# A ring of four raw weight chunks in place of three, and 37 universal tiles in place of 39

## The chip, the cores and the metric

The kernel runs on one core of a Trainium2 chip. A core has five engines that run side by side, each through its own queue of instructions: TensorE (PE, matrix products), VectorE (DVE), ScalarE (ACT), GpSimd (POOL) and SyncE (SP), which here only starts transfers (DMAs). They meet through semaphores: an instruction waits until what it reads has been written and what it overwrites has been read. On-chip memory is SBUF (128 partitions) and PSUM (eight banks, into which TensorE adds up). The metric is the time of one execution in microseconds (us); lower is better.

## The reference

A decoder trunk of two layers on 512 tokens of width 1024, in float32. Each layer has a mixer and a gated feed-forward network (FFN), each between two RMS norms:

```python
for i in range(DEPTH):                       # DEPTH = 2
    h = rms_norm(x, norm_g[i, 0])
    if i % 2 == 0:                           # differential attention and a short gated convolution
        p = h @ w_in_even[j]
        ...
        mix = jnp.concatenate([a_out, b_out], axis=-1) @ w_out_even[j]
    else:                                    # spatial gating unit
        mix = spatial_gating(h, w_in_odd[j], ..., w_out_odd[j])
    x = x + rms_norm(mix, norm_g[i, 1])
    h = rms_norm(x, norm_g[i, 2])
    f = (jax.nn.silu(h @ w_gate[i]) * (h @ w_up[i])) @ w_down[i]   # 1024 -> 2816 -> 1024
    x = x + rms_norm(f, norm_g[i, 3])
```

All weights lie in device memory and are read once.

## The kernel before, in words

**Weights.** SyncE loads all weights as chunks of at most 8 KB a partition (1 MB) into a ring of tiles `raw` (pool `rawp`, L83), in one fixed list `chunks`. `load` (L307 to L321) issues chunks until a limit of chunks whose parts have not all been read is met (L310). Chunks of the FFN are two transfers, a half of w_gate and a half of w_up, 512 KB each. A load can start once the tile that it takes over has been read, so a load waits for the release of the chunk that stood in that tile.

**Split.** Every weight piece is split into two reduced-precision parts: ScalarE casts the high part `whi` (L135), VectorE subtracts it from the raw piece to make the low part `wlo` (L136). TensorE then makes three products for each product wanted: high with high, high with low, low with high.

**FFN.** Gate and up are done in 11 units of 256 columns by a scheme with seven products in place of eight: the unit has two chunks ("a" and "b"), VectorE makes sums of their quarters (`wsum`, L263), and 7 pieces are multiplied, each 24 matmuls of 128x256 (L679). Results are combined on VectorE (L754, a PSUM bank and a copied tile, L759 on ScalarE makes the copy), then silu (L764, ScalarE) and the product (L765, VectorE) give `hidden`. The first three units start with two small pieces each, before all tokens are ready. The next use of a PSUM bank by TensorE can wait for the addition of L754. GpSimd in the meantime issues transfers that add up sums of w_down in device memory (`tsum`, L186), paced by L779; the down projection then runs on these in the same scheme.

**Pools.** The pool `ap` (tag "a", 4 KB a partition a tile) is shared by whi, wlo, wsum, the normed and turned activations, `hidden` and norm vectors. An allocation that finds all tiles in use waits for the reader of the oldest fitting one. Ring and pool together take 3 x 8 + 39 x 4 = 180 KB a partition.

**Order.** A scheduler sets the order on each engine when the kernel is built, from its own estimates of time; ScalarE's and VectorE's order is written out in the prologue alone, GpSimd's in the FFN. SyncE's queue follows the order in which loads are issued in the code.

Of the kernel before, what the change touches and what calls it, by code (L numbers as in the profile page):

```python
# [72 lines left out]
def trunk(  # L73
# [6 lines left out]
    nc = tc.nc  # L80
    pool = lambda name, bufs, **kw: ctx.enter_context(tc.tile_pool(name=name, bufs=bufs, **kw))
    const = pool("const", 1)
    rawp = pool("rawp", 3)  # L83
    ap_ = pool("ap", 39)
    tp = pool("tp", 8)
    sp = pool("sp", 24)
    ps_ = pool("ps", 8, space=bass.MemoryType.PSUM)
# [4 lines left out]
    def nm(base):  # L92
        n_made[0] += 1
        return f"{base}_{n_made[0]}"
# [19 lines left out]
    chunks, order = [], []  # L114
# [86 lines left out]
    class Unit:  # L201
# [46 lines left out]
        def sum(self, s):  # L248
            if s in self.sums:
                return self.sums[s]  # L250
            for before in self.NEEDS.get(s, []):
                self.sum(before)
            t = ap_.tile([P, 2, 4, P], F32, tag="a", name=nm("wsum"))
            if s == "s1":
                x, y, op = self.quarter("a", 1), self.quarter("b", 1), ALU.add
            elif s == "s2":
                x, y, op = self.sums["s1"], self.quarter("a", 0), ALU.subtract
            elif s == "s3":
                x = self.half["a"].tile[:, :, :, 0:P]
                y, op = self.quarter("a", 1), ALU.subtract  # L260
            else:
                x, y, op = self.quarter("b", 0), self.sums["s2"], ALU.subtract
            nc.vector.tensor_tensor(out=t, in0=x, in1=y, op=op)  # L263
            self.sums[s] = t
            return t
# [39 lines left out]
    n_loaded, n_split, ready = [0], [0], []  # L305

    def load(upto=1000):  # L307

        while n_loaded[0] < min(upto, len(chunks)):
            if sum(c.left > 0 for c in chunks[:n_loaded[0]]) >= 3:  # L310
                return
            c = chunks[n_loaded[0]]
            c.tile = rawp.tile(c.shape, F32, tag="raw", name=nm("raw"),
                               padded_shape=[P, 2048 // math.prod(c.shape[2:])] + c.shape[2:])
            for part, view in c.views:
                if n_loaded[0] >= 2:
                    nc.sync.dma_start(out=c.tile[part], in_=view)
                else:
                    for ks in (slice(0, 2), slice(2, 4)):
                        nc.sync.dma_start(out=c.tile[:, ks, :], in_=view[:, ks, :])  # L320
            n_loaded[0] += 1  # L321

    def ahead(n):

        while len(ready) < n and n_split[0] < len(order):
            key, need, make = order[n_split[0]]
            load()
            assert all(c.tile is not None for c in need)
            ready.append((key, make()))
            n_split[0] += 1  # L330
            load()
# [493 lines left out]
    for t in range(1, NT):  # L825
        load(t)
        nc.sync.dma_start(out=xs[t], in_=x[0, t * P:(t + 1) * P, :])
    with tc.manual_schedule(engines={mybir.EngineType.Activation, mybir.EngineType.DVE}):
# [62 lines left out]
        for i in range(2):  # L891
# [3 lines left out]
                            ap=[[1, P], [STRIP, 2], [1, 512]]))  # L895
# [298 lines left out]
```

## Time and profile before

| what | us |
|---|---|
| median of 3 runs (1069.45 to 1069.95) | 1069.6 |
| the profiled execution | 1071.01 |
| its span, first to last instruction | 1069.1 |
| TensorE busy in it | 1034.5 (97%) |
| VectorE busy | 812.6 (76%) |
| ScalarE busy | 552.1 (52%) |
| GpSimd busy | 191.4 (18%) |

The mean granted clock of TensorE is 0.99. The profiled execution lies 1.4 us above the median of the runs; its span leaves 1.9 us around it. The FFN's products run from 233 to 474 us in layer 0 and from 722 to 959 us in layer 1; in layer 0 the down projection follows until the second layer's mixer starts, in layer 1 it ends the kernel. In the timelines a number in brackets is the idle time of the engine just before an instruction, and behind the arrow stands what ended it. A matmul's duration overlaps with the next one's; what counts is the distance of two starts.

### The profile page before, as it was taken

Reading aid. Unit: us, or ns where it says so; the run is one execution under the profiler, and the core shown is the slowest. Engines: PE = TensorE matmul, PEld = TensorE weight load, DVE = VectorE, ACT = ScalarE, POOL = GpSimd, SP = SyncE. Lnnn points to the kernel's source line nnn. Section 1 sums busy time; section 2 is a strip of 40 time slices with the busy share of each in tenths; the row PEclk is TensorE's granted clock in tenths of the full one; section 3 lists DMA queues with packets and bytes.
Section 4 is the critical chain, followed back from the end, with each engine's and each line's share of the span. In section 5 each row is a group of like instructions: output and inputs, shape, how many; then the busy total and the mean of one; then the engine's idle time right before and its main releaser. Section 6 shows DMA issues by size and latency. Waiting matters only on the chain.

```text
span 1069.1 us, 16311 instructions
## 1 busy us (share of the span) xinstructions
PE 1034.5 (97%) x6395; PEld 923.1 (86%) x6395; DVE 812.6 (76%) x1179; ACT 552.1 (52%) x903; POOL 191.4 (18%) x259
## 2 busy tenths in 40 slices
PE   7999999998999999999999999998899999999997
PEld 5777778887899999998888788888899999998885
DVE  4466654489887996899978454679898797799974
ACT  4456453366453553584846433356455454474842
POOL 1012220011233333220000000010334343220000
PEclk7999999999999999999999999999999999999999
DMA  9231304326788798574744522414789799774741
GB/s 324 57 119 40 119 13 169 94 81 190 191 266 220 188 279 229 159 219 144 280 148 153 163 79 79 138 51 147 207 226 273 201 273 240 177 217 148 257 175 40
DMA packets 112526, 181.10 MB, mean 169 GB/s; under 512 B 5009, under 2 KB 77854, under 8 KB 110402
## 3 DMA queue, kind: packets, MB, share of 16 engines
q1 hardware_dynamic: 96578, 133.92, 38.0%
q0 software_dynamic: 15872, 46.14, 18.7%
q8 instruction: 50, 0.82, 0.3%
q14 instruction: 26, 0.21, 0.1%
HBM read 177.94 MB, written 48.24 MB: 212 GB/s over the span
## 4 chain that ended last, share of the span: by engine, by line
PE 72%; DVE 15%; DMA 4%; ACT 3%; issue 3%; POOL 1%; SPq 0%; DVEq 0%; POOLq 0%; ACTq 0%
PE ps L109 41%; PE ps L679 28%; DVE wlo L136 5%; DMA raw<-in_w_up_dram 3%; DVE wsum L263 3%; ACT whi L135 1%; POOL s L344 1%; DVE hTlo L432 1%; DVE h L503 1%; DVE t L754 1%; ACT j L491 1%; DVE x L552 1%; PE ps L952 1%; DMA raw<-in_w_in_even_dram 1%; DVE t L438 1%
## 5 line engine op out<-in xcount | busy, mean ns | idle before, releaser
L679 PE MATMUL ps<-hThi,whi 128*128 128x256 f32 x1232 | 275.1, 285 | 8.2 <-ACT whi L135 4.9
L679 PE MATMUL ps<-hThi,wlo 128*128 128x256 f32 x1232 | 275.0, 284 | 5.1 <-DVE wlo L136 5.1
L679 PE MATMUL ps<-hTlo,whi 128*128 128x256 f32 x1232 | 274.0, 284 | 1.3 <-DVE hTlo L432 1.3
L136 DVE TENSOR_TENSOR wlo<-raw,whi 128x1024 fp32r<-128x1024 f32 (+1 forms) x206 | 239.7, 1185 | 31.7 <-ACT whi L135 30.7
L135 ACT CAST whi<-raw 128x1024 fp32r<-128x1024 f32 (+1 forms) x206 | 203.6, 1018 | 27.3 <-DMA raw<-in_w_up_dram 7.8
L679 PEld LDWEIGHTS ps<-hThi,whi 128*128 128x128 f32 x1232 | 203.6, 192 | 10.6 <-ACT whi L135 5.9
L679 PEld LDWEIGHTS ps<-hThi,wlo 128*128 128x128 f32 x1232 | 204.0, 192 | 6.6 <-DVE wlo L136 6.5
L679 PEld LDWEIGHTS ps<-hTlo,whi 128*128 128x128 f32 x1232 | 203.8, 192 | 1.9 <-DVE hTlo L432 1.9
L135 ACT CAST whi<-wsum 128x1024 fp32r<-128x1024 f32 x88 | 90.1, 1045 | 57.7 <-DVE wsum L263 50.4
L109 PE MATMUL ps<-whi,wlo 128*128 128x512 f32 x308 | 119.9, 389 | 0.0
L109 PE MATMUL ps<-wlo,whi 128*128 128x512 f32 x308 | 119.8, 389 | 0.0
L109 PE MATMUL ps<-whi,whi 128*128 128x512 f32 x308 | 119.5, 390 | 0.2 <-DVE t L719 0.2
L779 POOL TENSOR_SCALAR pace<-t 128x1 f32<-128x1 f32 x96 | 74.2, 773 | 245.9 <-ACT t L764 172.4
L136 DVE TENSOR_TENSOR wlo<-wsum,whi 128x1024 fp32r<-128x1024 f32 x88 | 105.5, 1219 | 15.9 <-ACT whi L135 15.9
L344 POOL TENSOR_TENSOR s<-s,neg_half 128x1 f32<-128x1 f32 (+1 forms) x40 | 25.0, 627 | 486.8 <-DVE s L484 415.2
L754 DVE TENSOR_TENSOR t<-ps,t 128x512 f32<-128x512 f32 x88 | 58.4, 684 | 32.8 <-ACT t L759 17.6
L759 ACT COPY t<-ps 128x512 f32<-128x512 f32 x66 | 38.5, 583 | 86.2 <-PE ps L679 86.2
L109 PE MATMUL ps<-whi,a 128*128 128x512 f32 x256 | 79.9, 391 | 0.0
L186 POOL DMA_DIRECT2D tsum<-in_w_down_dram x72 | 68.4, 953 | 2.1 <-issue 0.8
L109 PEld LDWEIGHTS ps<-whi,whi 128*128 128x128 f32 x308 | 57.8, 188 | 12.6 <-issue 0.8
L109 PEld LDWEIGHTS ps<-wlo,whi 128*128 128x128 f32 x308 | 57.8, 188 | 11.9
L109 PEld LDWEIGHTS ps<-whi,wlo 128*128 128x128 f32 x308 | 57.8, 188 | 11.9
(143 smaller groups left out, 1485.8 us busy)
## 6 DMA issues: line engine op xcount, KB each, us to landing
tsum<-in_w_down_dram POOLq DMA_DIRECT2D x60, 512.0 KB, 7.0
raw<-in_w_gate_dram SPq DMA_DIRECT2D x44, 512.0 KB, 5.8
raw<-in_w_up_dram SPq DMA_DIRECT2D x44, 512.0 KB, 7.4
raw<-tsum SPq DMA_DIRECT2D x16, 1024.0 KB, 5.0
raw<-in_w_down_dram SPq DMA_DIRECT2D x12, 1024.0 KB, 5.9
raw<-in_w_in_even_dram SPq DMA_DIRECT2D x10, 1024.0 KB, 6.7
tsum<-tsum POOLq DMA_DIRECT2D x20, 512.0 KB, 5.9
raw<-in_w_in_odd_dram SPq DMA_DIRECT2D x8, 1024.0 KB, 5.4
```

The lines of the kernel that those rows point to most:

```text
L109: nc.tensor.matmul(out, lhsT, rhs, start=start, stop=stop, **kw)
L135: nc.scalar.copy(out=hi, in_=src)
L136: nc.vector.tensor_tensor(out=lo, in0=src, in1=hi.bitcast(F32), op=ALU.subtract)
L186: return [lambda to=to, of=of, g=g, op=op: nc.gpsimd.dma_start(out=to[:, g, :], in_=of[:, g, :], accum_op=op) for g in self.PAIRS for op, ...
L263: nc.vector.tensor_tensor(out=t, in0=x, in1=y, op=op)
L344: nc.gpsimd.tensor_tensor(out=y0[:, :n], in0=a, in1=neg_half[:, :n], op=ALU.pow)
L432: nc.vector.tensor_tensor(out=self.part(1, p, t), in0=src, in1=self.part(0, p, t).bitcast(F32), op=ALU.subtract)
L438: minus = lambda out, x, y: nc.vector.tensor_tensor(out=out, in0=x, in1=y, op=ALU.subtract)
L679: nc.tensor.matmul(bank[:, m * 256:(m + 1) * 256], piece[a][:, m, k, :], hT.at(b, p)[:, k, :], start=first and m == 0 and i == 0, stop=i = ...
L754: nc.vector.tensor_tensor(out=c, in0=x, in1=y, op=ALU.add)
L759: nc.scalar.copy(out=c, in_=x)
L779: nc.gpsimd.tensor_scalar(out=pace, in0=at[:, 0:1], scalar1=1.0, scalar2=None, op0=ALU.mult)
```

## The change

The ring has four tiles, `load` lets four chunks be unread, and the universal pool has 37 tiles: 4 x 8 + 37 x 4 = 180 KB again. Nothing is computed in another way.

```diff
@@ -80,8 +80,8 @@
     nc = tc.nc
     pool = lambda name, bufs, **kw: ctx.enter_context(tc.tile_pool(name=name, bufs=bufs, **kw))
     const = pool("const", 1)
-    rawp = pool("rawp", 3)
-    ap_ = pool("ap", 39)
+    rawp = pool("rawp", 4)
+    ap_ = pool("ap", 37)
     tp = pool("tp", 8)
     sp = pool("sp", 24)
     ps_ = pool("ps", 8, space=bass.MemoryType.PSUM)
@@ -307,7 +307,7 @@
     def load(upto=1000):
 
         while n_loaded[0] < min(upto, len(chunks)):
-            if sum(c.left > 0 for c in chunks[:n_loaded[0]]) >= 3:
+            if sum(c.left > 0 for c in chunks[:n_loaded[0]]) >= 4:
                 return
             c = chunks[n_loaded[0]]
             c.tile = rawp.tile(c.shape, F32, tag="raw", name=nm("raw"),
```

What the scheduler makes of it is shown at three places. On SyncE in the prologue (raw are the weight chunks of w_in_even, rows, lam_in, table and oh the small tables, strip_d and a the attention bias), before:

```order
L853 DMA rows<-in_conv_w_dram 12x128
L317 DMA raw_180<-in_w_in_even_dram 128x8x256
L854 DMA rows<-in_diff_subln_g_dram 1x128
L863 DMA lam_in<-in_diff_lambda_dram 128x256
L879 DMA table<-in_rel_bias_dram 32x4
L881 DMA oh<-in_one_hot_dram 32x512
L317 DMA raw_208<-in_w_in_even_dram 128x8x256
L889 DMA strip_d<-strip 4x640
```

and now:

```order
L317 DMA raw_154<-in_w_in_even_dram 128x8x256
L317 DMA raw_182<-in_w_in_even_dram 128x8x256
L317 DMA raw_210<-in_w_in_even_dram 128x8x256
L853 DMA rows<-in_conv_w_dram 12x128
L854 DMA rows<-in_diff_subln_g_dram 1x128
L863 DMA lam_in<-in_diff_lambda_dram 128x256
L879 DMA table<-in_rel_bias_dram 32x4
L881 DMA oh<-in_one_hot_dram 32x512
L889 DMA strip_d<-strip 4x640
```

Three loads stand ahead of the small tables now, one of them a chunk that before came behind the bias. On SyncE at the start of layer 0's FFN (g are norm vectors, raw the halves of gate and up), before:

```order
L317 DMA raw_2106<-in_w_gate_dram 128x4x128
L317 DMA raw_2106<-in_w_up_dram 128x4x128
L360 DMA g_2194<-in_norm_g_dram 128x1024
L360 DMA g_2196<-in_norm_g_dram 128x1024
L317 DMA raw_2205<-in_w_gate_dram 128x4x256
L317 DMA raw_2205<-in_w_up_dram 128x4x256
```

and now:

```order
L317 DMA raw_2013<-in_w_gate_dram 128x4x128
L317 DMA raw_2013<-in_w_up_dram 128x4x128
L317 DMA raw_2109<-in_w_gate_dram 128x4x256
L317 DMA raw_2109<-in_w_up_dram 128x4x256
L360 DMA g_2197<-in_norm_g_dram 128x1024
L360 DMA g_2199<-in_norm_g_dram 128x1024
```

The two norm vectors come behind one more chunk. On VectorE in the eighth of the units of layer 0 (wsum sums, wlo low parts, t additions of line 754, a the hidden products), before:

```order
L263 TENSOR_TENSOR wsum_4246<-wsum_4204,raw_3797 128x1024
L136 TENSOR_TENSOR wlo_4284<-wsum_4246,whi_4283 128x1024
L263 TENSOR_TENSOR wsum_4287<-raw_4002,wsum_4246 128x1024
L754 TENSOR_TENSOR t_4232<-ps_4108,t_4230 128x512
L754 TENSOR_TENSOR t_4236<-ps_4109,t_4230 128x512
L765 TENSOR_TENSOR a_3494<-t_4232 128x256
L136 TENSOR_TENSOR wlo_4321<-wsum_4204,whi_4320 128x1024
L765 TENSOR_TENSOR a_3499<-t_4236 128x256
```

and now:

```order
L263 TENSOR_TENSOR wsum_4249<-wsum_4207,raw_3759 128x1024
L136 TENSOR_TENSOR wlo_4287<-wsum_4249,whi_4286 128x1024
L754 TENSOR_TENSOR t_4235<-ps_4111,t_4233 128x512
L754 TENSOR_TENSOR t_4239<-ps_4112,t_4233 128x512
L765 TENSOR_TENSOR a_3497<-t_4235 128x256
L263 TENSOR_TENSOR wsum_4290<-raw_3800,wsum_4249 128x1024
L765 TENSOR_TENSOR a_3502<-t_4239 128x256
L136 TENSOR_TENSOR wlo_4324<-wsum_4207,whi_4323 128x1024
```

Two additions have moved ahead of the sum of line 263, and a product ahead of a split. The same kind of exchange stands in the last units of each layer and at the start of the down projections; TensorE exchanges single matmuls there, and GpSimd's order is as it was.

## Rows read from the trace of the kernel before

**Rows 1.** The page's first section: busy us, share of span, instructions.
```profile
PE 1034.5 (97%) x6395; PEld 923.1 (86%) x6395; DVE 812.6 (76%) x1179; ACT 552.1 (52%) x903; POOL 191.4 (18%) x259
```

**Rows 2.** Waits of TensorE, 240 to 480 us: total, times, longest.
```profile
PE ps L679 <- DVE wlo L136: 2.8, 4, 0.9
PE ps L679 <- DVE t L754: 2.8, 2, 1.8
PE ps L679 <- ACT whi L135: 2.2, 2, 1.8
```

**Rows 3.** Timeline, TensorE, 303 to 312 us: start, duration, instruction, idle before and releaser.
```profile
...
304.28 0.28 PE L679 MATMUL ps<-hThi,whi 128*128 128x256 f32 x1
304.40 0.28 PE L679 MATMUL ps<-hThi,wlo 128*128 128x256 f32 x1
306.46 0.47 PE L679 MATMUL ps<-hThi,whi 128*128 128x256 f32 x1 [1.79 <-DVE t L754]
...
```

**Rows 4.** Timeline, VectorE, 292 to 308 us.
```profile
...
301.71 1.22 DVE L136 TENSOR_TENSOR wlo<-raw,whi 128x1024 fp32r<-128x1024 f32 x1 [2.49 <-ACT whi L135]
...
305.13 1.28 DVE L754 TENSOR_TENSOR t<-ps,t 128x512 f32<-128x512 f32 x2
...
```

**Rows 5.** Timeline, ScalarE, 292 to 308 us.
```profile
...
300.63 2.00 ACT L135 CAST whi<-raw 128x1024 fp32r<-128x1024 f32 x2 [2.85 <-DMA raw<-in_w_up_dram]
...
```

**Rows 6.** Timeline, SyncE's queue, 255 to 320 us.
```profile
...
280.97 0.51 SPq L317 DMA_DIRECT2D raw<-in_w_up_dram  x1
...
292.38 0.51 SPq L317 DMA_DIRECT2D raw<-in_w_up_dram  x1
...
```

**Rows 7.** Windows: busy us of PE, PEld, DVE, ACT, POOL; granted clock, DMA share, GB/s.
```profile
306.46:310.10 3.64, 3.64 (x17) 3.64 (x18) 2.88 (x4) 1.14 (x2) 1.57 (x2) 0.53 0.26 23
```

**Rows 8.** Timelines of SyncE, ScalarE, VectorE and TensorE, 350 to 394 us.
```profile
...
358.21 0.51 SPq L317 DMA_DIRECT2D raw<-in_w_up_dram  x1
...
370.30 0.51 SPq L317 DMA_DIRECT2D raw<-in_w_up_dram  x1
...
380.06 1.05 ACT L135 CAST whi<-raw 128x1024 fp32r<-128x1024 f32 x1 [2.70 <-DMA raw<-in_w_up_dram]
...
381.15 1.23 DVE L136 TENSOR_TENSOR wlo<-raw,whi 128x1024 fp32r<-128x1024 f32 x1 [1.45 <-ACT whi L135]
...
390.56 0.39 PE L679 MATMUL ps<-hThi,whi 128*128 128x256 f32 x1 [0.97 <-DVE t L754]
...
```

**Rows 9.** Timelines of ScalarE and TensorE in layer 1, 780 to 797 us.
```profile
...
789.39 2.00 ACT L135 CAST whi<-raw 128x1024 fp32r<-128x1024 f32 x2 [1.67 <-DMA raw<-in_w_up_dram]
...
795.22 0.74 PE L679 MATMUL ps<-hThi,whi 128*128 128x256 f32 x4 [0.57 <-DVE t L754]
...
```

**Rows 10.** Windows at the start of each FFN stage (columns as in 7).
```profile
245.00:280.00 35.00, 29.63 (x231) 27.99 (x232) 33.41 (x43) 18.20 (x28) 6.82 (x9) 1.00 0.58 178
...
720.00:765.00 45.00, 38.74 (x302) 36.78 (x301) 42.70 (x67) 28.21 (x49) 6.79 (x10) 1.00 0.52 164
```

**Rows 11.** Timelines of VectorE and TensorE, 282 to 288 us.
```profile
...
283.76 1.23 DVE L263 TENSOR_TENSOR wsum<-raw,raw 128x1024 f32<-128x1024 f32 x1 [0.26 <-DMA raw<-in_w_up_dram]
...
287.39 0.38 PE L679 MATMUL ps<-hThi,wlo 128*128 128x256 f32 x1 [0.88 <-DVE wlo L136]
...
```

**Rows 12.** Waits of ScalarE, 392 to 480 us.
```profile
...
ACT whi L135 <- PE ps L679: 6.5, 4, 2.6
...
```

**Rows 13.** Windows in the steady part of each FFN stage.
```profile
392.00:480.00 88.00, 88.00 (x700) 86.27 (x698) 73.66 (x86) 50.16 (x68) 25.07 (x38) 1.00 0.77 204
797.00:960.00 163.00, 163.00 (x1345) 162.28 (x1344) 138.32 (x158) 88.43 (x121) 56.87 (x77) 1.00 0.85 230
```

**Rows 14.** Timeline, VectorE, 403 to 412 us.
```profile
...
407.66 1.23 DVE L263 TENSOR_TENSOR wsum<-raw,wsum 128x1024 f32<-128x1024 f32 x1 [0.57 <-PE ps L679]
...
```

**Rows 15.** Timelines of SyncE and TensorE in the prologue.
```profile
...
21.88 0.38 SPq L317 DMA_DIRECT2D raw<-in_w_in_even_dram  x1
...
44.38 0.23 PE L856 MATMUL ps<-ident,rows 16*128 16x16 f32 x1
...
```

## The prediction

> **What bounds the kernel now.** The page's first section comes first: TensorE is busy 97% of the span, so what can be won at all is the time in which it stands still or runs at a lower clock [rows 1]. Next come the waits of TensorE in the feed-forward (FFN) stage; the reader is to see which engine ended each wait [rows 2]. In layer 0 one of the two largest groups, 2.8 us in two waits, is on the VectorE addition of line 754; the rest is on splits (whi, wlo). The list of idle stretches and their engines is only the outside of it: behind each wait I went back one engine at a time, in the timelines of TensorE, VectorE, ScalarE and SyncE, until a wait had no engine behind it. Where that ends at a DMA of raw weights, a chunk that starts one step sooner can help; where it ends at a VectorE that had no pause, it can't.
>
> The larger of the two line-754 waits: TensorE stands still for 1.79 us before 306.46 [rows 3]. The addition that it waits for starts at 305.13, behind a VectorE that had itself lost 2.49 us at 301.71 to a missing whi [rows 4], which ScalarE could not cast because the chunk's second half (in_w_up) had not landed: idle 2.85 us before 300.63 [rows 5]. That half was issued at 292.38, about 8.2 us before [rows 6]. After the stall TensorE is granted half of its clock: in the 3.64 us from 306.46 the mean grant is 0.53, and 17 matmuls are done [rows 7].
>
> The smaller: 0.97 us before 390.56 [rows 8]. ScalarE sits 2.70 us before 380.06 for in_w_up, VectorE then 1.45 us for ScalarE. The half was issued at 370.30, so it took 9.8 us [rows 8]. Layer 1 has the same picture in small: 0.57 us before 795.22, behind 1.67 us of ScalarE on in_w_up before 789.39 [rows 9].
>
> The start of both FFN stages is different. From 245 to 280 us VectorE is busy 33.41 of 35 us, and from 720 to 765 it is 42.70 of 45 us [rows 10]. TensorE's waits there are on wlo and whi that VectorE makes as fast as it can. No load changes that.
>
> **The change part by part.** *The ring.* A load now waits for the release of the chunk four before it, not three. Each FFN chunk is one of two for a unit of seven pieces, so releases come in pairs. The load issued at 292.38 therefore takes the place of the one issued at 280.97, 11.4 us sooner, and the one at 370.30 that of 358.21, 12.1 us sooner [rows 6, 8]. Even with the 9.8 us landing of the slower one they are there at about 291 and 368, before ScalarE wants them (near 297.8, which is 300.63 less 2.85, and 377.4).
>
> What is late next? At the first place VectorE can go on at 301.71 - 2.49 = 299.2; its row of work up to the addition lasts 3.4 us (301.71 to 305.13), so the two additions run from 302.6 to 303.9, where before they ended at 306.4. TensorE's last matmul before the stall starts at 304.40 and the next would follow 0.12 us later [rows 3], so 0.6 us of slack are left and the 1.79 us go whole. At the second place VectorE gains its 1.45 us, and the addition ends 0.5 us before it is due: the 0.97 us go whole [rows 8]. At the third, 1.67 us of ScalarE stand against 0.57 us: gone [rows 9].
>
> *The clock.* If the stall at 306 goes, the half-clock stretch goes with it: 17 matmuls at the spacing of 0.12 us seen just before take 2.04 us, they took 3.64, so 1.60 us [rows 3, 7]. Bounds: 0, if something else lowers it, and 1.60.
>
> The rows show a clock drop behind the 1.79 us stall, but none behind a wait of 1.8 us for whi in the FFN's start, where the grant stays 1.00 from 245 to 280 [rows 2, 10]. So the sum takes one drop. [...]
>
> *Another few tenths.* At 283.76 VectorE waits 0.26 us for in_w_up, and that passes through its chain to the 0.88 us stall at 287.39: 0.26 us [rows 11]. Bounds 0 and 0.88; the chain is VectorE's own otherwise, so the lower price.
>
> *The pool.* 37 tiles in place of 39: whi, wlo, sums and hidden share it, and an allocation waits only when all are in use. That is so at the end of the FFN: between 392 and 480 ScalarE's casts wait 6.5 us in four waits for TensorE to give a tile back [rows 12]. With two tiles fewer each such wait is for a release up to one piece (24 matmuls, 24 x 0.12 = 2.9 us) later. It costs nothing while the splits run ahead of TensorE, and they do: it is busy 88.00 of 88 us there and 163.00 of 163 in the same stretch of layer 1 [rows 13]. That row shows that the lead is above zero, not how large it is. Bounds: 0, or one piece for each of four waits, 11.5 us; I take 0, since even four waits of up to 2.6 us cost TensorE nothing today.
>
> *The order.* In the late FFN the additions of line 754 move ahead of a sum or split that waits for a tile. At 407.66 the sum (line 263) waits 0.57 us for a tile and the two additions stand behind it [rows 14]; they would start up to 1.7 us sooner, the sum some 1.3 us later (the two additions, 1.28 us in [rows 4]). TensorE waits for neither there: 0, with bounds of 1.3 us each way. At the start, three loads pass ahead of the five small tables (conv weights, bias table, one-hot). The last of them waits for the release at which SyncE issued a load before, 21.88, so the tables go out behind that, against a first use at 44.38 [rows 15]: 0, since 22 us of other matmuls lie between; it would cost only if they took longer than that. The norm vectors go behind one pair of loads, and are out when the pair's chunk has been released; that is the release at which SyncE issued a load before them, so it is 0 too. Nothing else is passed in SyncE's queue, and GpSimd's order stays.
>
> **Sum.** 1.79 + 1.60 + 0.97 + 0.57 + 0.26 = 5.19 us. The profiled execution took 1071.01 us (span 1069.1 and 1.9 around it): 1065.8. The median of the runs shown, 1069.6, lies 1.4 below the profiled one; from it, 1064.4. I forecast 1064.6.
>
> **Rivals.**
> 1. *The pool stops TensorE* (slower). Place: the last units of each FFN stage, where ScalarE already waits for tiles [rows 12]. If the lead of a piece there is under 2.9 us, TensorE gets a stall of up to 2.9 us with a clock drop of 1.6 behind it, in each layer: 2 x 4.5 = 9.0, against 5.2 gained: 1069.6 + 3.8 = 1073.4. It decides from a stall of 2.6 us per layer in all. For it: two tiles are worth one piece. Against it: TensorE's idle time there is zero.
> 2. *VectorE stays late* (same). The loads land, but VectorE, busy 84 to 95% of the FFN [rows 10, 13], is bound by sums and splits, and the two stalls come back a piece later as waits for wlo. Only the 0.57 and part of the rest are won, some 1.2 us: 1068.4. For it: the start of the stage is of that kind throughout [rows 10]. Against it: 2.49 and 1.45 us of pause that VectorE demonstrably had [rows 4, 8].
> 3. *Transfers collide* (same). The earlier load runs beside GpSimd's accumulating transfers of w_down and takes as much longer as it starts earlier. The half issued at 292.38 needed 8.2 us, the one at 370.30 9.8 us; to undo 11.4 us it would need about 20. Time: 1069.6, or slightly less. The Trainium skill ("DMA: Bandwidth & Descriptors", SWDGE vs HWDGE vs iDMA) says that the DMA engines alternate between the queues fed by GpSimd and by SyncE. By it a load beside a burst of sums is slowed to about half its rate, never held up, which fits the rows; no run here shows it alone.
> 4. *More is won* (faster). Part of the 0.88 us at 287 and of the start stalls goes too, and waits that lengthen ScalarE's chain vanish: another 3 us at most, 1061.6.
>
> **How the numbers follow.** A change under 0.2%, 2.1 us, can't be told from none here. Forecast (gain 3 to 6.5 us): 0.58. Rival 4: 0.10. Rivals 2 and 3 with gains under 2.1: 0.15 and 0.04; a small pool cost that eats most of the gain: 0.04. Rival 1: 0.09. So faster 0.69, same 0.22, slower 0.09. The range reaches from 1061.8 (rival 4) to 1070.0, which leaves out rival 1 and the far end of 4. The likeliest case's own range is 1063.1 to 1066.6.
>
> **What would show it.** Right: no TensorE wait on line 754 near 304 and 388 and none near 794; a granted clock of 1.00 through 300 to 320; ScalarE's waits for in_w_up in the FFN at nearly none; in_w_up issued near 281 and 358. Right on the pool: longer waits of ScalarE's casts for TensorE in the late FFN, and TensorE still without pause from 392 on. Wrong: any new wait of TensorE on whi or wlo between 392 and 480 or between 797 and 960, a second half-clock stretch, or landings of raw chunks of 15 us and more.

## The result and the profile after

The changed kernel takes 1064.1 us (median of 4 runs, 1062.89 to 1065.65) against 1069.78 for the kernel before (4 runs, 1069.45 to 1072.3): a ratio of 0.9944, with a 95% interval of 0.9927 to 0.9961, 5.7 us. Forecast were 1064.6. The profiled execution took 1065.65 us, its span is 1063.9; before they were 1071.01 and 1069.1.

The page's first section and the waits of TensorE from 240 to 480 us, in the order of [rows 1, 2]:

```profile
PE 1032.9 (97%) x6395; PEld 922.0 (87%) x6395; DVE 812.0 (76%) x1179; ACT 552.4 (52%) x903; POOL 199.5 (19%) x259
```

```profile
PE ps L679 <- DVE wlo L136: 2.6, 4, 0.9
PE ps L679 <- ACT whi L135: 2.2, 2, 1.8
...
```

The group on line 754 is gone, the other two stand where they stood (2.6 against 2.8 us, 2.2 against 2.2). How it went is read from the place near 306: timelines of SyncE, ScalarE, VectorE and TensorE (the places of [rows 6, 5, 4, 3]), then the window from 300 to 320 us.

```profile
...
281.62 0.51 SPq L317 DMA_DIRECT2D raw<-in_w_up_dram  x1
...
297.09 2.96 ACT L135 CAST whi<-raw 128x1024 fp32r<-128x1024 f32 x3
...
298.35 2.35 DVE L136 TENSOR_TENSOR wlo<-raw,whi 128x1024 fp32r<-128x1024 f32 x2
...
303.00 1.29 DVE L754 TENSOR_TENSOR t<-ps,t 128x512 f32<-128x512 f32 x2
...
304.75 0.28 PE L679 MATMUL ps<-hThi,wlo 128*128 128x256 f32 x1
304.87 0.28 PE L679 MATMUL ps<-hThi,whi 128*128 128x256 f32 x1
...
```

```profile
300.00:320.00 20.00, 20.00 (x169) 20.00 (x169) 19.24 (x22) 10.10 (x15) 12.52 (x14) 1.00 0.93 285
```

The half of w_up that was issued at 292.38 starts at 281.62. ScalarE casts three pieces in a row from 297.09 without a pause, VectorE goes from 298.35 to 304.3 with hardly one, and the two additions end 0.6 us before TensorE's first matmul that needs them, at 304.87, which follows its predecessor by 0.12 us. The grant is 1.00 throughout, where the same window of the kernel before has 0.91.

Start by start, the 6395 matmuls of the two profiled executions can be laid against each other. The changed kernel is 0.65 us late when the FFN begins, then gains 0.30 at 287, 1.94 at the stall near 306 (1.79 of wait and the slower first matmul), 1.60 over the next 17 matmuls, 1.24 near 390 and 0.84 near 795; all other steps are 0.11 us or less and nearly cancel. The sum is 5.9, less 0.65 makes the 5.2 by which the span is shorter.

The 0.65 us arise before 24 us, where TensorE runs at half clock in both. Executions of one kernel differ by more than that: in the two profiles of the kernel before, the FFN's first wait for h ended at 245.70 and 246.95, in the two of the changed kernel at 246.36 and 245.15.

What the pool does is in ScalarE's waits and in two windows, in the order of [rows 12, 13]:

```profile
...
ACT whi L135 <- PE ps L679: 11.2, 5, 4.2
ACT whi L135 <- PE ps L109: 2.4, 2, 1.4
...
```

```profile
392.00:480.00 88.00, 88.00 (x682) 85.59 (x682) 73.86 (x84) 48.33 (x65) 23.56 (x35) 1.00 0.77 208
797.00:960.00 163.00, 163.00 (x1323) 161.34 (x1323) 136.66 (x157) 87.31 (x120) 53.74 (x73) 1.00 0.84 226
```

ScalarE waits 11.2 us in five waits for TensorE to return a tile, where it waited 6.5 in four, and 2.4 us more at the down projection's first pieces. TensorE was busy all the time all the same. It has fewer matmuls in the same stretch (682 against 700) because the changed kernel is 4.4 us ahead there and so does more of the down projection, whose matmuls are longer (128x512).

### The profile page after: what moved, and what is told of

Read it like the earlier page. It is cut to its first block, busy times and chain, and to the rows that moved or that the text cites. A ratio compares the mean times of both kernels' runs of the same rounds, so it can differ in the third digit from the quotient of the medians.

```text
span 1063.9 us, 16330 instructions
## 1 busy us (share of the span) xinstructions
PE 1032.9 (97%) x6395; PEld 922.0 (87%) x6395; DVE 812.0 (76%) x1179; ACT 552.4 (52%) x903; POOL 199.5 (19%) x259
## 4 chain that ended last, share of the span: by engine, by line
PE 80%; DVE 11%; ACT 3%; issue 2%; DMA 2%; POOL 1%; SPq 0%; DVEq 0%; POOLq 0%; ACTq 0%
PE ps L109 41%; PE ps L679 35%; DVE wlo L136 3%; DVE wsum L263 1%; POOL s L344 1%; DVE hTlo L432 1%; ACT whi L135 1%; DVE h L503 1%; ACT j L491 1%; PE ps L952 1%; DMA raw<-in_w_in_even_dram 1%; DVE x L552 1%; PE ps L1138 1%; PE ps L513 1%; DMA raw<-in_w_up_dram 1%
## 5 line engine op out<-in xcount | busy, mean ns | idle before, releaser
L779 POOL TENSOR_SCALAR pace<-t 128x1 f32<-128x1 f32 x96 | 82.1, 856 | 235.7 <-ACT t L764 169.0
L109 PEld LDWEIGHTS ps<-whi,whi 128*128 128x128 f32 x308 | 57.8, 188 | 12.6 <-issue 0.8
```

The source lines that it names most:

```text
L109: nc.tensor.matmul(out, lhsT, rhs, start=start, stop=stop, **kw)
L779: nc.gpsimd.tensor_scalar(out=pace, in0=at[:, 0:1], scalar1=1.0, scalar2=None, op0=ALU.mult)
```

## The experiments

Kernels that ran together share their runs of the kernel before, so it is the ratios that are compared across the rows. Times are medians. The second run of the changed kernel has no wait of TensorE on line 754, and none from 392 to 474 us.

| kernel | us | ratio to before, 95% interval |
|---|---|---|
| changed | 1064.1 | 0.9944 (0.9927 to 0.9961) |
| changed, again | 1064.44 | 0.9939 (0.9923 to 0.9954) |
| ring 3, pool 37 | 1070.74 | 1.0003 (0.9993 to 1.0013) |
| ring 4, pool 37, limit left at 3 | 1064.96 | 0.9948 (0.9935 to 0.996) |
| changed, one late chunk in unit 3 | 1069.4 | 0.9989 (0.9978 to 1.0) |
| changed, one late chunk in unit 7 | 1067.43 | 0.9977 (0.9962 to 0.9992) |
| ring 4, pool 35 | 1066.56 | 0.9961 (0.9947 to 0.9974) |
| ring 5, pool 35 | 1066.33 | 0.9962 (0.9949 to 0.9974) |
| ring 4, pool 33 | 1081.94 | 1.0103 (1.0086 to 1.0121) |
| before, sums of w_down later | 1076.71 | 1.0045 (1.0024 to 1.0066) |
| before, again | 1070.41 | 0.9999 (0.9985 to 1.0012) |
| changed, six sums on GpSimd | 1083.2 | 1.0118 (1.0104 to 1.0131) |

The theory in all of them is that of the prediction: the gain comes from a load that starts one release sooner and so doesn't hold up ScalarE, VectorE and TensorE in turn, and the smaller pool and the new order cost nothing.

**Ring of three with the smaller pool.**

```diff
-    ap_ = pool("ap", 39)
+    ap_ = pool("ap", 37)
```

> Ring of three and limit of three as before, pool of 37 tiles: VectorE, ScalarE and TensorE have the changed kernel's order, SyncE has the old one. Theory (the gain is the earlier load): the same as before, 1069.7 us within 1, with the stall of about 1.8 us on line 754 near 306, the half clock behind it and the stall near 390 of about 1.0. Rival A (the gain is the new order of additions in the late FFN that the smaller pool brings): near the changed kernel, 1064 to 1065, no line-754 stalls. Rival B (the pool costs something that the ring pays back): over 1071, with new waits of TensorE between 392 and 480.

It has the changed kernel's order on VectorE, ScalarE, TensorE and GpSimd and the old queue on SyncE, and it takes as long as the kernel before. So the exchange of additions and sums in the late FFN is the pool's doing, and the two together are worth nothing with a ring of three. The stall near 306 was there. Timeline of TensorE, and the window behind:

```profile
...
308.15 0.39 PE L679 MATMUL ps<-hThi,whi 128*128 128x256 f32 x1 [2.22 <-DVE t L754]
...
```

```profile
308.15:311.90 3.75, 3.75 (x18) 3.75 (x19) 2.89 (x4) 1.19 (x2) 1.57 (x2) 0.54 0.29 55
```

The stall near 390 was not, which the theory had missed. There the half was issued at 372.02 and landed 4.9 us later, where [rows 8] have 9.8. What differs is the order of the load and a transfer of GpSimd: below.

**The limit in the code.** Line 310 left at 3, ring 4, pool 37.

```diff
-            if sum(c.left > 0 for c in chunks[:n_loaded[0]]) >= 4:
+            if sum(c.left > 0 for c in chunks[:n_loaded[0]]) >= 3:
```

> Ring of four tiles and pool of 37, but line 310 left at three. Theory: the release of the tile decides when a load starts, not the limit in the code, so this is the changed kernel: 1064.5 us within 1, no stall on line 754, no half clock in the FFN, the second chunk of unit 3 issued near 281. Rival: the limit decides, and it is the kernel before: 1070 us, with the stall near 306.

It is the changed kernel in time, and the half of unit 3 was issued at 280.35. Of the change's three lines this one does next to nothing: the load's wait is on its tile. In SyncE's queue the limit moves one load of the prologue, which goes behind the small tables again, and the time doesn't show it.

**One late chunk.** In the kernel with the limit at 3, a copy of two elements a partition from a sum of VectorE into the chunk's tile makes its load wait for that sum; all other loads stay early. The copy itself takes 0.16 us of VectorE, which doesn't wait before it. For unit 3 it is

```diff
+            if c in guards:
+                unit, name = guards[c]
+                nc.vector.tensor_copy(out=c.tile[:, :, 0, 0:1], in_=unit.sums[name][:, :, 0, 0:1])
...
+    guards = {units0[3].half["b"]: (units0[2], "s3")}
```

> The changed kernel with one single chunk made late: the second chunk of unit 3 in layer 0 (the one that landed at 300.6 in the kernel before) can start only when VectorE has made the last sum from the chunk three before it. Theory: the stall on line 754 near 306 comes back, 1.8 to 3.5 us since a half of the next chunk now goes ahead of it, and a half-clock stretch of 1.6 us behind it: 3.4 to 5.1 us over the changed kernel, 1067.5 to 1069.2 us. Rival A (the order makes the gain): no stall, 1064 to 1065. Rival C (the clock drop is unrelated to the stall): the stall alone, 1.8 to 3.5 us, clock 1.00 behind it.

Timelines of ScalarE and TensorE and the window (source lines below the copy are four higher, so 754 reads 758):

```profile
...
301.98 2.00 ACT L135 CAST whi<-raw 128x1024 fp32r<-128x1024 f32 x2 [4.60 <-DMA raw<-in_w_up_dram]
...
307.81 0.39 PE L683 MATMUL ps<-hThi,whi 128*128 128x256 f32 x1 [3.08 <-DVE t L758]
...
```

```profile
307.81:311.60 3.79, 3.79 (x21) 3.79 (x22) 2.88 (x4) 1.24 (x2) 1.56 (x2) 0.63 0.33 43
```

One late chunk of 1 MB brings the stall back, here 3.08 us since a half of the next chunk went ahead of it, and the slow stretch behind it. Of the ratio's 0.0056 it takes 0.0045, 4.8 us: the stall and, as forecast, some 1.6 us of slow clock are 4.7. So the two terms are a matter of this one load. The stall is longer than the one that the change removed, so it shows the mechanism and not its exact price; 1069.4 us is 0.2 above what was expected.

The same for unit 7, `guards = {units0[7].half["b"]: (units0[6], "s2")}`:

> The same for the second chunk of unit 7 in layer 0 (the one awaited at 380.06 in the kernel before). Theory: a stall on line 754 near 386 comes back, 1.0 to 2.7 us: 1065.1 to 1066.8 us if the clock holds as it did there before, 1.6 more if a stall of about 1.8 us is what lets it fall. Rival A: no stall, 1064 to 1065.

```profile
...
377.64 1.05 ACT L135 CAST whi<-raw 128x1024 fp32r<-128x1024 f32 x1 [3.33 <-DMA raw<-in_w_up_dram]
...
388.14 0.39 PE L683 MATMUL ps<-hThi,whi 128*128 128x256 f32 x1 [1.12 <-DVE t L758]
...
```

```profile
388.14:391.80 3.66, 3.66 (x30) 3.66 (x31) 3.37 (x5) 2.08 (x3) 2.08 (x2) 1.00 0.48 152
```

A stall of 1.12 us and no clock drop in the profile. The median is 3 us above the changed kernel's, more than the stall; its runs spread from 1065.2 to 1072.55, and the profiled one, 1067.17 us, shows no other new wait. What the slower ones have is left open.

**Why a chunk needs 8 to 10 us.** The kernel before, with GpSimd's sums of w_down in layer 0 put off until unit 3, two at a time from there; the order on the other engines is unchanged.

```diff
+                if layer == 0 and now[0] < EARLY:
+                    owed[0] += 1
+                    return
                 sums.pop(0)()
+                if owed[0]:
+                    owed[0] -= 1
+                    sums.pop(0)()
```

> The kernel before (ring of three, pool of 39) with GpSimd's sums of w_down in layer 0 put off until unit 3, two at a time from there; the order on the other four engines is as before. It asks why a chunk issued at 292.4 needed 8.2 us. Theory (it shares the DMA engines with GpSimd's accumulating transfers): alone it lands in 4 to 6 us, by 298.4, ScalarE's wait before 300.63 shrinks from 2.85 to under 1 us, and the stall near 306 and its half clock go, 1066 to 1068 us, unless the denser sums later make a new wait near 330 to 400. Rival (the transfer itself takes that long): the wait and the stall stay, 1069 to 1071 us.

Timeline of ScalarE, at the cast that waited 2.85 us in [rows 5] and at the one of [rows 8]; then TensorE at the second:

```profile
...
296.47 2.95 ACT L135 CAST whi<-raw 128x1024 fp32r<-128x1024 f32 x3
...
382.09 1.04 ACT L135 CAST whi<-raw 128x1024 fp32r<-128x1024 f32 x1 [7.22 <-DMA raw<-in_w_up_dram]
...
383.67 0.39 PE L679 MATMUL ps<-hThi,whi 128*128 128x256 f32 x1 [2.88 <-ACT t L759]
...
```

With a ring of three and the load issued at 292.13, the half lands 5.1 us later, where it took 8.2 in the kernel before; it is there when ScalarE gets to it at about 297.5 (three casts in 2.95 us from 296.47), and the stall near 306 is gone. Where the sums are dense in its place a half lands 14.2 us after its issue at 367.79, ScalarE waits 7.22 us for it and TensorE 2.88. The packets of the two queues show why. In the kernel before, SyncE's queue moved nothing from 292 to 295 us while GpSimd's moved 0.40 MB, and from 296 to 300 SyncE's moved 1.45 MB with GpSimd's all but empty; with the sums put off, GpSimd's queue moved nothing from 292 to 297.3 and SyncE's 1.35 MB. So how long a chunk takes depends on what GpSimd has in flight; the total got worse, as the denser stretch costs more than the quiet one saves. The theory's figure, 1066 to 1068, was missed for that reason, which the expectation had named as its exception; its mechanism was right.

**The kernel before, again.**

> The kernel before once more, for a second profile of it. Theory: the stall near 306 is there again, 1.8 to 2.3 us with a half-clock stretch behind it, since its chunk is issued after the 14 us that its predecessor's work takes. The stall near 390 need not be: in the run with a ring of three and a pool of 37 it was absent, with SyncE's issue 0.35 us ahead of a GpSimd transfer that was 0.15 us ahead of SyncE in the first profile. If it is present again at 0.97 us, that explanation is weakened.

```profile
...
307.67 0.38 PE L679 MATMUL ps<-hThi,whi 128*128 128x256 f32 x1 [1.72 <-DVE t L754]
...
390.39 0.38 PE L679 MATMUL ps<-hThi,whi 128*128 128x256 f32 x1 [1.10 <-DVE t L754]
...
```

```profile
300.00:320.00 20.00, 18.28 (x152) 18.08 (x151) 17.16 (x21) 10.93 (x15) 8.59 (x12) 1.00 0.85 259
```

The stall of 1.72 us is there, the clock drop is not. The stall near 390 is there as well. In both profiles that have it GpSimd issued a transfer of sums just ahead of the gate half (369.73 against SyncE's 369.88, and 369.51 against 369.59); in the run that lacks it, behind (371.96 against 371.61). Being first is not enough, though. In the changed kernel's profile and in the one with a late chunk in unit 3 SyncE's gate half was 0.14 and 0.16 us ahead (366.75 against 366.89, 370.73 against 370.89), and the half of w_up behind it still took 8.9 and 9.7 us, as where GpSimd was first (9.7 and 9.8). It took 6.0 us in the changed kernel's second profile and 4.9 with ring 3 and pool 37, where SyncE was 0.31 and 0.35 us ahead. So the landing goes with a few tenths of a us between two issues; no run sets them on purpose, and the cause stays argued.

**Smaller pools.** Ring 4, pool 33 and 35, and ring 5 with 35.

> Ring of four, pool of 33 tiles in place of 37: asks how much lead the pieces have. By the forecast's first rival a pool this small must show: ScalarE's casts wait for TensorE far longer than 11.2 us between 392 and 480, and TensorE stalls in the late FFN of both layers, 1 to 3 us each with a half-clock stretch where over about 1.8: 1067 to 1073 us. If the lead (10 us and more, at most places) covers four further tiles too: 1064 to 1065 us, with no wait of TensorE there.

> Ring of four, pool of 35: half way between 37, where TensorE did not wait in the late FFN, and 33, where it did for 7.9 us in layer 0 and ran at half clock besides. Theory (a threshold: the lead absorbs the later releases until it is used up): first stalls of TensorE on whi and wlo near 440 and 450, 1 to 3 us in layer 0, none in layer 1, 1065 to 1069 us. Rival (cost in proportion to the tiles taken away, and so already something at 37): about half of the 17 us that 33 cost, 1072 to 1074 us.

> Ring of five, limit of five, pool of 35. Against the run with a ring of four and the same pool it shows the fifth tile alone. Theory: no wait of ScalarE for in_w_up is left with four, so the fifth gives nothing: equal to the pool-35 run within 1 us. Rival (loads are still late somewhere, at 287 for one): 1 to 2 us less than that run, the 0.59 us stall near 287 gone.

Waits of TensorE from 392 to 480 us at 33 tiles, then a window of it, and the waits at 35 tiles:

```profile
PE ps L679 <- DVE wlo L136: 4.2, 5, 1.2
PE ps L679 <- ACT whi L135: 3.2, 3, 1.1
PE ps L109 <- DVE wlo L136: 0.5, 1, 0.5
```

```profile
440.00:460.00 20.00, 15.45 (x107) 14.65 (x108) 10.64 (x12) 8.57 (x11) 2.60 (x4) 0.91 0.30 79
```

```profile
PE ps L679 <- DVE wlo L136: 0.2, 1, 0.2
```

At 33 TensorE waits nine times, 7.9 us, and the grant falls to 0.83 from 430 to 450 and to 0.91 from 440 to 460; the kernel loses 17 us against the changed one, 9 more than the most that was expected. Waits and clock make up about 11 of the 17; for the rest the views name no wait. At 35 there is one wait of 0.2 us there and another of 0.17 later, and the median is 1.6 us up; laid against the run with 37 tiles, start by start, the rest comes in steps of 0.1 to 0.4 us between 430 and 580 us and in layer 1's down projection, where the views show no wait. What those are is left open. So the cost is not in proportion to the tiles taken away: it has a knee, somewhere about 35 tiles. The prediction's first rival named the right place and the right engine; with 37 it doesn't come. The fifth ring tile gives nothing: with pool 35 it is 1066.33 against 1066.56, and the wait near 287 is 0.54 us in both.

**Sums on GpSimd.** The third sum of each of the first three units of a layer.

```diff
-            nc.vector.tensor_tensor(out=t, in0=x, in1=y, op=op)
+            engine = nc.gpsimd if s in self.SPARE else nc.vector
+            engine.tensor_tensor(out=t, in0=x, in1=y, op=op)
```

> The changed kernel with the third sum of each of the first three units of a layer (line 263, six in all) made by GpSimd in place of VectorE. Theory (the stalls at the start of each FFN stage come from VectorE's work, not from loads): VectorE has 3 x 1.14 us less to do between 250 and 290 and between 735 and 780, and TensorE's waits there, 5.2 and 5.7 us without the ones for h, shrink by 1 to 3 us each: 1059 to 1063 us. Rival (GpSimd, which also paces the sums of w_down, is slower at it and its transfers come later, or VectorE slows down beside it): same or slower, 1064 to 1067 us, with new waits on the third sum.

It lost 19 us against the changed kernel, far more than its rival had allowed for. Timelines of GpSimd and VectorE, and TensorE's wait after (source lines below are three higher):

```profile
...
268.06 2.61 POOL L266 TENSOR_TENSOR wsum<-raw 128x1024 f32<-128x1024 f32 x1
...
268.32 3.42 DVE L266 TENSOR_TENSOR wsum<-raw,raw 128x1024 f32<-128x1024 f32 x1
...
272.88 0.58 PE L682 MATMUL ps<-hThi,whi 128*128 128x256 f32 x1 [2.53 <-ACT whi L135]
...
```

GpSimd needs 2.6 us for the sum that VectorE makes in 1.2, and a VectorE sum that starts beside it takes 3.42 us in place of 1.22; a subtraction for wlo, at 286.74, took 4.34. The time that VectorE was to be spared it spends standing. The Trainium skill ("SBUF — State Buffer", SBUF: two separate sides) says that a VectorE operation with two SBUF inputs and a GpSimd one that reads SBUF exclude each other for a whole instruction; the trace agrees: the two slow ones end 1.07 and 1.09 us after GpSimd's, about one operation of VectorE later. The clock adds to it, which nobody had expected: from 245 to 300 and from 740 to 780 us the grant is 0.84 and 0.87, where the changed kernel has 1.00 in both. That is some 28 us at half clock, and at the price of the stretch near 306 (1.60 us lost in 3.64) up to 12 of the 19 us. That the stage's start is bound by VectorE's work this run can't confirm, since it didn't lessen it.

## Why the prediction was right

- *The ring: right.* Issue at 281.62 (forecast 280.97, in a span that runs 0.65 late) and at 355.08 (forecast 358.21, by then 3.1 us ahead), no wait of ScalarE for in_w_up from 290 to 480, additions from 303.0 to 304.3 where 302.6 to 303.9 was worked out. The slack of 0.6 us came out as worked out. The landing was longer than allowed for: with the limit at 3, the half issued at 280.35 landed 12.6 us later, not 9.8, and still some 4 us before ScalarE wanted it.
- *The stalls: right*, 1.79, 0.97 and 0.57 us, with the restored stalls of the single late chunks as the proof for the first two. The one near 390 is less fixed than I took it: both profiles of the kernel before have it, the one with ring 3 and pool 37 lacks it.
- *287: right.* From 0.88 to 0.59 us, 0.29 for the 0.26 forecast.
- *The clock: right in the profiled execution, wrong as a constant.* Four profiles here have the stall near 306 in a kernel with a late chunk: in three a half-clock stretch follows, in one it doesn't. The wait of 1.83 us near 256 stands in twelve of the thirteen profiles, and in ten of them nothing falls behind it, as the prediction read it; in the second profile of the changed kernel, shown here, and with the late chunk of unit 3 the clock does fall:

```profile
255.00:264.00 9.00, 7.95 (x51) 7.75 (x52) 9.00 (x13) 5.53 (x9) 2.34 (x1) 0.81 0.40 117
```

  The mean is steadier. Over the runs of one session the granted clock was 0.9910 before (23 runs) and 0.9932 after (6): times twice the span, 19.2 and 14.5 us at half clock, 4.7 us less. At the price of the stretch near 306 (1.60 us lost in 3.64) that is about 2 us gained, so a term of 1.6 us was of the right size. Why 5.7 to 6.5 us were measured where 5.2 were forecast stays open: the means also hold the half-clock stretch at the kernel's start, from 0 to 26 us a grant of 0.74 in six of the thirteen profiles and 0.80 in seven, with kernels of either ring in both.
- *The pool: right at zero*, and its threshold lies close by. The lead was of unknown length, as the prediction said: two more tiles away and it begins to run out.
- *The order and the queue: right at zero.* The tables went out from 23.45 us, first used at 45.02; with the limit at 3 one of the three loads goes back behind them and the time stays.
- *Rivals.* 1 (the pool stops TensorE) is real at 33 tiles. 2 (VectorE stays late) didn't come: it had the pauses. 3 (transfers collide): the collision is what makes the chunk slow, and the earlier load does take longer (12.6 us with the limit at 3, in place of 8.2), but it starts 11 us sooner. That a load beside the sums runs at about half its rate and is never held up, which the prediction found to fit the rows, does not fit the trace of the kernel before: from 287 to 290 us SyncE's queue moved 0.23 MB against GpSimd's 0.46, from 282 to 284 only 0.03 against 0.34, and from 292 to 295 nothing. 4: 287 gained its third, the rest of the start nothing.
- *Slips.* The chances add up to 0.68, 0.23 and 0.09, not 0.69, 0.22 and 0.09. And of the two kinds of piece that TensorE waits for in the stage's start VectorE makes wlo alone; whi is ScalarE's cast, which there waits for sums of VectorE.

That the sum came within half a us of the median was in part luck: its prices come from one profile, which had both the clock drop and the stall near 390, and of the two other profiles with the old loads each lacks one of them.

## What to carry to other kernels

Follow a wait back until it ends at something that no engine was late for; here it was three engines deep, and the engine that the idle list named (VectorE) had itself been waiting. Here a deeper prefetch paid for the few transfers that land late, not for the mean, and one tile more was all there was to have. When a pool pays for it, look at whether the consumer ever stood still, and find how near the knee is before taking more.

## What the runs showed of the hardware that was not expected

Two matmul waits of the same length (1.79 and 1.72 us, at the same place in the same kernel) were followed by a half-clock stretch (17 matmuls long) in one execution and by none in another: one profile prices a clock drop only for itself. Two VectorE operations of 1.22 us took 3.42 and 4.34 us beside a GpSimd sum of 2.6 to 2.8 us, so the sums given to GpSimd here cost VectorE more than they spared it. And a SyncE load issued at 292 us moved nothing until 295 while GpSimd's accumulating transfer moved 0.40 MB: beside such a transfer a load can stand still, and not only slow down.
